# RWKV scan: wide operand products, 16-row inverses, a merge one group ahead and preparations between a group's halves

## The chip, the cores and the metric

The kernel runs on one core of one Trainium2 chip. The metric is the device time of one launch in microseconds (us). Matrix products run on TensorE (PE; its weight loads are PEld), elementwise work on VectorE (DVE), ScalarE (ACT) and GpSimd (POOL), transfers are issued by SyncE (SP).

## The reference, cut to what matters

The kernel computes four layers over 512 latent tokens and 256 context tokens of width 1024 in float32. The change touches one of them, the RWKV-7 mixer, and in it the scan over tokens, for 16 heads of 64 channels and for both directions:

```python
def step(S, inp):
    w_t, k_t, v_t, kk_t, a_t = inp[:5]
    sa = jnp.einsum('bhvk,bhk->bhv', S, -kk_t)
    S = (S * w_t[:, :, None, :] + sa[..., None] * (kk_t * a_t)[:, :, None, :]
         + v_t[..., None] * k_t[:, :, None, :])
    y = jnp.einsum('bhvk,bhk->bhv', S, inp[5]) if len(inp) == 6 else None
    return S, y
```

The context is scanned first and gives the start state of the latents; only latent steps give an output y. The kernel works in chunks of 64 tokens: within a chunk the steps become a unit lower triangular 64x64 system for each head, whose inverse is built once, and the state goes from chunk to chunk by matrix products.

## The kernel before

`rwkv_scan` handles 24 units. A unit is one direction d, one half h of the channels (8 heads, as 4 pairs on 128 partitions) and one stretch of 128 tokens (two chunks, j = 0 and 1): 8 systems of 2 heads. Units 0 to 7 are context, 8 to 23 latents. Two units (h = 0, 1) of the same direction make a pair; there are 12 pairs, and the direction alternates from pair to pair. Four steps make up the work:

- `prepare(g, d, h)` loads five operands (four for the context), runs a prefix sum on DVE (L1673), three exponentials on ACT, and the products of the operands with the decays on DVE: `W[.., 0]` (L1681, two of 64x512), `BK` (L1693 and L1694, eight of 64x256 for one unit, since each head's half is written into its own block of a zero-padded tile), `W[.., 1]` (L1697, latents only). Then, for j and for each two head pairs a0, eight matmuls (L1710, contraction over 128 partitions, half of them zeros) fill two PSUM banks, `pgB` and `pgK`, out of a ring of four; DVE takes them out under a mask (L1712 once, L1716 twice, 256 columns each for latents) and ACT takes out the rest (L1713, L1717). Last, ACT copies the 32x32 diagonal blocks, negated, to `diag` (L1719).
- `inverse(g, d)` transposes the pair's 32x32 blocks on DVE (L1726, 128x1024) and inverts them by forward substitution in `base_inverse`: 30 steps of two operations on POOL (L769, L770), or on DVE for pairs 1 and 11 (`n in (3, 23)`, n being the last unit of the pair).
- `merge(g, d, tv)` transposes the inverses twice on DVE (L1732, L1733, 128x1024), and builds the 64x64 inverse from the two 32x32 ones with 32 matmuls (L1742), a negation on ACT (L1744), copies on DVE and ACT (L1746), 32 matmuls (L1749) and copies on ACT (L1751).
- `consume(g, d, h, j)` is the recurrence: matmuls L1772, a copy on ACT (L1774), L1777, ACT (L1779), then L1786 and L1787 for the context or L1795 and L1796 for latents, the output on ACT (L1801), a transpose on PE (L1805) and the new state on DVE (L1782).

The operands of six units (`W`, `B`, `w`) are kept in a ring (`NS = 6`). Program order is written out at the end of `rwkv_scan`: after a start (units 0 to 4 prepared, pair 0 merged), each pair k is consumed, first j = 0 and then j = 1 for both units, then pair k+1 is merged, then units 2k+6 and 2k+7 are prepared and the pair of them goes to its inverse. A planner at compile time orders each engine's queue by the times that it estimates, with program order as the priority; on the chip each queue runs in that order. Units 0 and 1 are prepared while the projection of v still runs (its weights are split on POOL, L168); the other units come after it, from about 2596 us, when the tiles of the projection are free. The stage after the scan (`rwkv_out`) begins with the sum of the two directions' outputs (L1878).

Of the kernel before, what the change touches and what calls it, by code (L numbers as in the profile page):

```python
# [28 lines left out]
_CST = ["ident", "ones", "bd64", "cen"]  # L29
# [32 lines left out]
class K:  # L62
# [694 lines left out]

    def base_inverse(self, X, vector=False, pool=None):

        nc = self.nc  # L760
        v = X.rearrange("p (r c) -> p r c", r=32)
        nc.gpsimd.memset(X[:, 0:1024:33], 1.0)
        tt = nc.vector.tensor_tensor if vector else nc.gpsimd.tensor_tensor
        for k in range(1, 31):
            n = 31 - k
            t = (pool or self.pb).tile([128, 256], F32, name="binv", tag=f"binv{int(vector)}", bufs=2)
# [829 lines left out]
    def rwkv_scan(self):  # L1596
# [5 lines left out]
        pool = self.pb  # L1602
        reset, masks = self.cp[0], self.rr[1].rearrange("p (a b) -> p a b", a=2)
# [4 lines left out]
        i4 = lambda n, sh=None: pool.tile(sh or [128, 1024], F32, name=n, tag="i4", bufs=4)  # L1608
        BK = [pool.tile([128, 4, 2, 128], F32, name=f"BK{i}") for i in range(2)]

        diag = [pool.tile([128, 32, 32], F32, name=f"Ld{d}") for d in range(2)]
        X0 = pool.tile([128, 1024], F32, name="X0")
# [11 lines left out]
        for t in BK:  # L1624
            nc.gpsimd.memset(t, 0.0)
        for t in diag:
            nc.gpsimd.memset(t[:, 16:32], 0.0)
# [3 lines left out]
        for i, ch in enumerate((d, h) for d in range(2) for h in range(2)):  # L1631
            work[ch] = [g4[i], *h2((self.x[2:4] + self.cp[2:4])[i]), h2(self.x[4 + i // 2])[i % 2].rearrange("p a t -> p (a t)").rearrange("p (b h t) -> p b h t", b=2, h=2)]
# [8 lines left out]
        seen = set()  # L1641
# [4 lines left out]
        def prepare(g, d, h):  # L1646
# [3 lines left out]
            w4 = lambda hh, x: W[half[hh], :, x, hh, :]  # L1650
            src = lambda n, o: R[n][4 * h:4 * h + 4, :, o * 128:(o + 1) * 128].rearrange("c p t -> p c t")
            t = {}
            for n in (f"sig{d}", "kk", f"b{d}", f"kd{d}"):
                t[n[:2]] = e2("i" + n)
# [9 lines left out]
            W, B = s["W"], s["B"]  # L1664
            if 4 * g + 2 * d + h < NS:
# [3 lines left out]
            if not ctx and id(s) not in seen:  # L1669
                seen.add(id(s))  # L1670
                nc.gpsimd.memset(W[:, :, 1], 0.0)
# [7 lines left out]
            v4 = lambda x, hh: o(x[half[hh]]).rearrange("p (u t) -> p u t", u=8)  # L1679
            for hh in range(2):  # L1680
                nc.vector.tensor_tensor(out=w4(hh, 0), in0=v4(kk, hh), in1=v4(We, hh), op=ALU.mult)  # L1681
            nc.scalar.copy(s["w"].unsqueeze(2), u8(Wi)[:, :, 63:64])
            for j in range(2):
                k = 1 - j if d else j
                ts = slice(64 * k, 64 * k + 64)
                us = slice(j, 8, 2)
                bk = BK[nbk[0] % len(BK)]
                nbk[0] += 1
                r1 = (lambda x: x[:, ::-1, ::-1]) if d else (lambda x: x)
                r0 = (lambda x: x[:, ::-1]) if d else (lambda x: x)  # L1690
                for hh in range(2):
                    ps = half[hh]
                    nc.vector.tensor_tensor(out=bk[ps, :, hh, 0:64], in0=r1(b[ps, :, ts]), in1=r1(iW[ps, :, ts]), op=ALU.mult)  # L1693
                    nc.vector.tensor_tensor(out=bk[ps, :, hh, 64:128], in0=r0(kd[ps, :, ts]), in1=r0(iW[ps, :, ts]), op=ALU.mult)  # L1694
                if j == 0 and not ctx:
                    for hh in range(2):
# [298 lines left out]
def prep(I):  # L1995
    A = {}
# [164 lines left out]
```

## Time and profile before

| | us |
|---|---|
| median of 3 runs (3607.12 to 3620.38) | 3610.18 |
| profiled execution, its own time | 3611.94 |
| its span, first to last instruction | 3610.2 |
| the scan after the projection of v, 2596 to 3126 us of the span | 530 |

The profile's time and span are 1.7 us apart and within 0.05% of the median. Times in the rows below are microseconds from the start of the span unless marked ns. A row of the stretches gives its bounds and length, then for PE, PEld, DVE, ACT and POOL the busy time (x instructions), then the granted TensorE clock as a share of full speed, the busy share of the DMA engines and GB/s. A row of the grouped instructions gives line, engine, operation, tiles (out<-in), shape, count, then total busy time and the mean of one in ns, then the idle time of the engine before them and who ended it. A row of the timeline gives start, duration, engine, line, operation, tiles, shape and count, with the idle time before it in brackets.

### The profile page before, as it was taken

The page shows a single profiled execution, that of the slowest core. Times are in us where ns is not written, and L with a number is a line of the kernel's source. Part 1 is how long each engine was busy: PE and PEld are TensorE (multiplying, and loading weights), DVE is VectorE, ACT ScalarE, POOL GpSimd, SP SyncE. Part 2 cuts the span into 40 slices and gives each one's busy share as a digit, 9 for nine tenths or more (in the row PEclk, how much of TensorE's full clock was granted, in tenths as well). Part 3 has the DMA queues.
Part 4 walks back from the last instruction along what each step waited for, and adds up shares of the span by engine and source line. Part 5 has one row for each costly group of instructions (what it writes and reads, how often), then busy time and mean ns, then how long its engine had stood idle before and what let it go on. Part 6 is the DMA issues. An engine that isn't in the chain of part 4 may idle for free. (4 is left out here: it accounts for less than half of the span.)

```text
span 3610.2 us, 52987 instructions
## 1 busy us (share of the span) xinstructions
PE 3125.1 (87%) x20190; PEld 2483.5 (69%) x20190; DVE 2068.2 (57%) x3360; ACT 1446.5 (40%) x2766; POOL 1850.5 (51%) x1676
## 2 busy tenths in 40 slices
PE   5679895888989898999999998898867788789998
PEld 2258684766777686787888886665756667568886
DVE  7976845547667676674071415746489888540002
ACT  3247533333212446644212123356345555442223
POOL 6742631356556555534434334456647777165553
PEclk9789996999999899999999999888968888889999
DMA  6312357734332251122142512355412232412222
GB/s 218 122 64 72 114 206 238 216 115 142 120 108 99 82 164 47 32 75 88 59 175 94 179 68 81 115 200 200 126 51 82 73 80 75 152 58 100 99 95 81
DMA packets 265462, 412.14 MB, mean 114 GB/s; under 512 B 73716, under 2 KB 155252, under 8 KB 265208
## 3 DMA queue, kind: packets, MB, share of 16 engines
q1 hardware_dynamic: 265208, 408.75, 34.5%
q8 instruction: 160, 2.62, 0.3%
q14 instruction: 94, 0.77, 0.1%
HBM read 331.34 MB, written 70.25 MB: 111 GB/s over the span
## 5 line engine op out<-in xcount | busy, mean ns | idle before, releaser
L168 POOL TENSOR_TENSOR wlo<-wraw,whi 128x1024 fp32r<-128x1024 f32 (+1 forms) x269 | 660.2, 2456 | 897.6 <-ACT whi L172 871.4
L172 ACT CAST whi<-wraw 128x1024 fp32r<-128x1024 f32 (+1 forms) x269 | 278.1, 1036 | 862.1 <-PE pmm L192 760.4
L191 PE MATMUL pmm<-hxh,whi 128*128 128x512 f32 x1320 | 532.0, 406 | 20.3 <-ACT hxh L262 9.4
L192 PE MATMUL pmm<-hxl,whi 128*128 128x512 f32 x1320 | 532.3, 404 | 13.5 <-POOL hxl L168 13.5
L193 PE MATMUL pmm<-hxh,wlo 128*128 128x512 f32 x1320 | 529.3, 401 | 0.0
L284 DVE SCALAR_TENSOR_TENSOR mjunk<-mraw,cv 128x1024 bf16<-128x1024 f32 x224 | 351.5, 1569 | 62.8 <-DMA mraw<-in_mod_w 37.7
L191 PEld LDWEIGHTS pmm<-hxh,whi 128*128 128x128 f32 x1320 | 254.0, 193 | 80.3 <-ACT hxh L262 12.3
L192 PEld LDWEIGHTS pmm<-hxl,whi 128*128 128x128 f32 x1320 | 253.0, 192 | 72.9 <-POOL hxl L168 19.9
L193 PEld LDWEIGHTS pmm<-hxh,wlo 128*128 128x128 f32 x1320 | 253.6, 192 | 55.7 <-issue 0.7
L191 PE MATMUL pmm<-hch,whi 128*128 128x256 f32 x760 | 221.3, 291 | 9.9 <-ACT hch L262 6.5
L192 PE MATMUL pmm<-hcl,whi 128*128 128x256 f32 x760 | 220.5, 290 | 7.9 <-POOL hcl L168 7.8
L193 PE MATMUL pmm<-hch,wlo 128*128 128x256 f32 x760 | 220.1, 290 | 0.0
L1371 DVE TENSOR_TENSOR sg<-sg,pmm 128x512 f32<-128x512 f32 x44 | 30.2, 687 | 325.1 <-PE pmm L193 307.9
L770 POOL TENSOR_TENSOR X<-X,binv 128x30 f32<-128x30 f32 (+4 forms) x330 | 199.1, 604 | 23.9
L769 POOL TENSOR_TENSOR binv<-X 128x30 f32<-128x30 f32 (+4 forms) x330 | 187.7, 570 | 23.8
L191 PEld LDWEIGHTS pmm<-hch,whi 128*128 128x128 f32 x760 | 148.3, 195 | 19.8 <-ACT hch L262 8.9
L192 PEld LDWEIGHTS pmm<-hcl,whi 128*128 128x128 f32 x760 | 147.7, 194 | 16.4 <-POOL hcl L168 11.2
L193 PEld LDWEIGHTS pmm<-hch,wlo 128*128 128x128 f32 x760 | 148.3, 195 | 1.4 <-issue 0.8
L1710 PE MATMUL pgB<-W,BK 128*64 128x192 f32 (+1 forms) x768 | 106.5, 357 | 42.0 <-ACT B L1713 17.1
L191 PE MATMUL pmm<-lh,whi 128*128 128x512 f32 (+1 forms) x320 | 117.8, 370 | 23.1 <-ACT lh L1444 15.7
L191 PE MATMUL pmm<-hh,whi 128*128 128x512 f32 x352 | 137.8, 392 | 0.0
L192 PE MATMUL pmm<-hl,whi 128*128 128x512 f32 x352 | 137.8, 392 | 0.0
(546 smaller groups left out, 7639.9 us busy)
## 6 DMA issues: line engine op xcount, KB each, us to landing
mraw<-in_mod_w SPq DMA_DIRECT2D x96, 512.0 KB, 3.5
wraw<-in_wg SPq DMA_DIRECT2D x44, 512.0 KB, 3.4
wraw<-in_wu SPq DMA_DIRECT2D x44, 512.0 KB, 3.4
wraw<-in_e_w_in SPq DMA_DIRECT2D x32, 512.0 KB, 3.3
wraw<-in_o_w_in SPq DMA_DIRECT2D x32, 512.0 KB, 3.2
wraw<-in_wd SPq DMA_DIRECT2D x32, 512.0 KB, 3.4
mraw<-in_e_mod_w SPq DMA_DIRECT2D x24, 512.0 KB, 3.9
mraw<-in_o_mod_w SPq DMA_DIRECT2D x24, 512.0 KB, 5.1
```

Of the source, the lines that this page charges most:

```text
L168: self.nc.gpsimd.tensor_tensor(out=out, in0=in0, in1=in1, op=op)
L172: self.nc.scalar.copy(hi, src)
L191: nc.tensor.matmul(ps, lhsT=a[0], rhs=b[0], start=start, stop=False)
L192: nc.tensor.matmul(ps, lhsT=a[0], rhs=b[1], start=False, stop=False)
L193: nc.tensor.matmul(ps, lhsT=a[1], rhs=b[0], start=False, stop=stop)
L284: nc.vector.scalar_tensor_tensor(out=junk, in0=raw, scalar=1.0, in1=cv, op0=ALU.mult, op1=ALU.mult, accum_out=out[:, c:c + 1])
L769: tt(out=tv, in0=v[:, k + 1:, k:k + 1].to_broadcast(sh), in1=v[:, k:k + 1, :k].to_broadcast(sh), op=ALU.mult)
L770: tt(out=v[:, k + 1:, :k], in0=v[:, k + 1:, :k], in1=tv, op=ALU.add)
L1371: nc.vector.tensor_tensor(out=t, in0=t, in1=ps, op=ALU.mult)
L1710: nc.tensor.matmul(view(p)[half[q], a], lhsT=bk[:, a0 + a, hh, o:o + 64], rhs=rhs, start=True, stop=True)
```

## The change

1. **Operand products.** `BK` becomes one unpadded tile for a unit; eight DVE products of 64x256 become two of 128x512. The zero fills of `W`, `BK` and `diag` on POOL go.
2. **Fills.** The matmuls that fill `pgB` and `pgK` contract over 64 partitions only; a tile takes two banks and holds all four head pairs, and the ring of four single banks becomes two double ones. For each j, 16 matmuls, then one masked product of B and two of W on DVE, each 512 columns wide for latents, and three copies on ACT.
3. **Inverse.** The substitution runs on 16x16 blocks: `base_inverse(..., 16)` takes 14 steps on POOL, for all pairs, on tiles of 256 columns. Ahead of it stand a DVE transpose of 128x512 and one DVE operation that picks blocks.
4. **Merge.** Two ACT copies, two DVE transposes of 128x512, then 160 added matmuls of 32x32x32 in three rounds, with four DVE operations between and behind them that build the 32x32 inverses from the 16x16 ones. The steps from 32 to 64 stay.
5. **Consume.** The first product is eight matmuls of 64 columns that need no extraction of diagonal blocks (one ACT copy less); the order of the latents' last product alternates the halves of the output.
6. **Order.** The merge of pair k+2 is emitted between the two halves of pair k+1, one group earlier; the preparation of unit 2k+6 stands ahead of the first half of pair k+1 and that of 2k+7 behind the merge.
7. Loads of `sig` and `kk` get a ring of their own (four buffers beside five). A constant block (`sub`, 128x128) is added to one load at the start.

```diff
-    def base_inverse(self, X, vector=False, pool=None):
+    def base_inverse(self, X, vector=False, pool=None, m=32):
...
-        for k in range(1, 31):
-            n = 31 - k
+        for k in range(1, m - 1):
+            n = m - 1 - k
...
-        BK = [pool.tile([128, 4, 2, 128], F32, name=f"BK{i}") for i in range(2)]
+        BK = [pool.tile([128, 2, 8, 64], F32, name=f"BK{i}") for i in range(2)]
...
-                nc.gpsimd.memset(W[:, :, 0:3:2], 0.0)
...
+            bk = BK[nbk[0] % len(BK)]
+            tt(out=pj(bk[:, 0]), in0=run(b), in1=run(iW), op=ALU.mult)
+            tt(out=pj(bk[:, 1]), in0=lie(kd), in1=lie(iW), op=ALU.mult)
+            if not ctx:
+                for hh, q in enumerate(half):
+                    tt(out=pj(w4(hh, 1)), in0=run(r)[q], in1=run(Wi)[q], op=ALU.mult)
...
             for j in range(2):
+                pB, pK = self.bank("g", "pgB"), self.bank("g", "pgK")
+                vB, vK = (p.rearrange("p (a x) -> p a x", a=4) for p in (pB, pK))
+                for a in range(4):
+                    u = 2 * a + j
+                    for i, p in enumerate((vB, vK)):
+                        for hh in range(2):
+                            nc.tensor.matmul(p[half[hh ^ i], a, 0:n], lhsT=bk[half[hh], i, u], rhs=W[half[hh], u, 0:3:step, hh], start=True, stop=True)
+                bu = B[:, j:8:2]
+                tt(out=bu[:, :, 0:64 * sm], in0=vB[:, :, 0:64 * sm], in1=m4(masks[:, 0]), op=ALU.mult)
+                nc.scalar.copy(bu[:, :, 128:192], vB[:, :, 64 * sm:n])
                 for hh in range(2):
-                    nc.vector.tensor_tensor(out=bk[ps, :, hh, 0:64], in0=r1(b[ps, :, ts]), in1=r1(iW[ps, :, ts]), op=ALU.mult)
-                    nc.vector.tensor_tensor(out=bk[ps, :, hh, 64:128], in0=r0(kd[ps, :, ts]), in1=r0(iW[ps, :, ts]), op=ALU.mult)
...
+                    q = half[1 - hh]
+                    tt(out=W[q, j:8:2, 0:sm, hh, :], in0=x64(vK[q, :, 0:64 * sm]), in1=x64(m4(masks[q, d])), op=ALU.mult)
+                    nc.scalar.copy(W[q, j:8:2, 2, hh, :], vK[q, :, 64 * sm:n])
...
         def inverse(g, d, vector=False):
-            nc.vector.transpose(out=xv, in_=diag[d].rearrange("p u c -> p c u"))
-            self.base_inverse(X, vector, pool)
+            nc.vector.transpose(out=Xt, in_=by(diag[d]))
+            nc.vector.scalar_tensor_tensor(out=X, in0=Xt[:, :, 0:16], scalar=even, in1=Xt[:, :, 16:32], op0=ALU.mult, op1=ALU.add)
+            self.base_inverse(X.rearrange("p r c -> p (r c)"), vector, pool, 16)
...
+        def merge(g, d, X):
+            for b, m in enumerate((even, odd)):
+                nc.scalar.activation(out=z[:, :, 16 * b:16 * b + 16], in_=X, func=AF.Copy, scale=m)
+            nc.vector.transpose(out=by(U), in_=z)
+            nc.vector.transpose(out=flat(Tc), in_=flat(U))
+            for u in range(16):
+                for q, _ in blk:
+                    nc.tensor.matmul(v16(pa)[q, u], lhsT=diag[d][q, u], rhs=Tc[q, u], start=True, stop=True)
+            tt(out=Y1, in0=v16(pa), in1=corner.unsqueeze(1).to_broadcast([128, 16, 32]), op=ALU.mult)
+            for u in range(16):
+                for q, _ in blk:
+                    nc.tensor.matmul(v16(pb)[q, u], lhsT=Y1[q, u], rhs=U[q, u], start=True, stop=True)
+            for u in range(16):
+                for q, _ in blk[::2]:
+                    nc.tensor.matmul(v16(pc)[q, u], lhsT=U[q, u], rhs=Y1[q, u], start=True, stop=True)
+            for q, _ in blk[::2]:
+                tt(out=Tc[q], in0=Tc[q], in1=v16(pc)[q], op=ALU.add)
+            tt(out=U, in0=U, in1=v16(pb), op=ALU.add)
...
-                nc.tensor.matmul(p4[:, a], lhsT=W[:, u, 0].rearrange("p h t -> p (h t)"), rhs=hv[:, a].rearrange("p h e -> p (h e)"), start=True, stop=True)
+                for hh, q in enumerate(half):
+                    nc.tensor.matmul(p4[q, a], lhsT=W[:, 2 * a + j, 0, hh], rhs=hv[:, a, hh], start=True, stop=True)
...
-                    tv[n // 2] = inverse(*pair(n // 2), n in (3, 23))
+                    tv[n // 2] = inverse(*pair(n // 2))
...
         for k in range(12):
-            for j in range(2):
-                for n in (2 * k, 2 * k + 1):
-                    consume(*unit(n), j)
...
-            join(k + 1)
             ahead(2 * k + 6)
+            both(k + 1, 0)
+            join(k + 2)
             ahead(2 * k + 7)
+            both(k + 1, 1)
...
-    with k.phase("rwkv_b", "right"), k.psum("ps_g", g=4):
+    with k.phase("rwkv_b", "right"), k.psum("ps_g", g=(2, 2)):
```

`ahead(n)` prepares unit n and, for odd n, issues the pair's inverse; `join(n)` merges pair n; `both(k, j)` consumes half j of pair k.

## Rows read from the trace of the kernel before

**Rows 1.** Busy time of each engine in four stretches of the scan.

```profile
2596.00:2708.00 112.00, 66.74 (x1040) 56.18 (x1040) 95.33 (x219) 59.21 (x172) 49.21 (x83) 0.70 0.26 71
2708.00:2800.00 92.00, 72.11 (x1040) 60.21 (x1040) 85.38 (x152) 50.93 (x147) 67.31 (x111) 0.84 0.30 82
2800.00:3064.00 264.00, 212.07 (x2788) 172.75 (x2788) 223.41 (x384) 149.50 (x440) 206.94 (x355) 0.88 0.29 76
3064.00:3126.00 62.00, 51.25 (x820) 46.08 (x820) 37.12 (x87) 29.39 (x81) 5.33 (x15) 0.89 0.39 117
```

**Rows 2.** Grouped instructions of DVE, shapes apart, 2800 to 3064 us.

```profile
L1716 DVE TENSOR_TENSOR W<-pgK,r 64x256 f32<-64x256 f32 x96 | 40.2, 420 | 18.0 <-PE pgK L1710 10.1 <-ACT W L1717 5.9
L1694 DVE TENSOR_TENSOR BK<-ikd,x 64x256 f32<-64x256 f32 x44 | 27.2, 618 | 0.8 <-PE pgK L1710 0.7
L1693 DVE TENSOR_TENSOR BK<-ib,x 64x256 f32<-64x256 f32 x44 | 23.9, 542 | 8.4 <-ACT x L1678 7.7
L1712 DVE TENSOR_TENSOR B<-pgB,r 128x256 f32<-128x256 f32 x48 | 20.1, 420 | 2.5 <-PE pgB L1710 1.3 <-PE pch L1795 0.2
L1681 DVE TENSOR_TENSOR W<-ikk,isig 64x512 f32<-64x512 f32 x22 | 18.7, 848 | 1.2 <-PE pch L1772 1.0
...
L1746 DVE COPY B<-Uc 32x256 f32<-32x256 f32 x24 | 14.8, 618 | 0.4
...
L1732 DVE STREAM_TRANSPOSE Tc<-X 128x1024 f32<-128x1024 f32 x6 | 12.5, 2080 | 0.2
```

**Rows 3.** The same view, 2620 to 2660 us, where POOL is almost at rest.

```profile
L1716 DVE TENSOR_TENSOR W<-pgK,r 64x128 f32<-64x128 f32 x20 | 5.7, 287 | 0.5
L1693 DVE TENSOR_TENSOR BK<-ib,x 64x256 f32<-64x256 f32 x10 | 4.2, 417 | 0.3
...
L1681 DVE TENSOR_TENSOR W<-ikk,isig 64x512 f32<-64x512 f32 x3 | 2.2, 720 | 0.0
...
L1746 DVE COPY B<-Uc 32x256 f32<-32x256 f32 x4 | 1.1, 286 | 0.1
```

**Rows 4.** Timeline of DVE behind the scan: a 128x512 product that reads PSUM.

```profile
3146.42 0.69 DVE L1852 TENSOR_TENSOR rstd<-rstd,pyc 128x512 f32<-128x512 f32 x1 [4.47 <-ACT rstd L1887]
```

**Rows 5.** Grouped instructions of DVE, 2596 to 3126 us: the two inverses that run there.

```profile
L769 DVE TENSOR_TENSOR binv<-X 128x30 f32<-128x30 f32 (+14 forms) x60 | 24.1, 402 | 1.7
...
L770 DVE TENSOR_TENSOR X<-X,binv 128x30 f32<-128x30 f32 (+14 forms) x60 | 22.8, 380 | 1.7
```

**Rows 6.** Waits of DVE, 2596 to 2708 us: total, times, longest.

```profile
DVE Tc L1732 <- POOL X L770: 7.2, 1, 7.2
DVE W L1681 <- POOL W L1666: 5.4, 2, 5.1
```

**Rows 7.** Grouped instructions of POOL, shapes apart, 2800 to 3064 us.

```profile
L770 POOL TENSOR_TENSOR X<-X,binv 128x58 f32<-128x58 f32 x12 | 6.1, 508 | 0.9
...
L769 POOL TENSOR_TENSOR binv<-X 128x30 f32<-128x30 f32 x12 | 3.9, 341 | 0.5
```

**Rows 8.** Timeline of PE at the full granted clock: fills, and bursts of small products.

```profile
2845.76 0.33 PE L1710 MATMUL pgB<-W,BK 128*64 128x192 f32 x1
2845.77 0.33 PE L1710 MATMUL pgK<-W,BK 128*64 128x192 f32 x1
2845.92 0.33 PE L1710 MATMUL pgB<-W,BK 128*64 128x192 f32 x1
...
3093.28 0.68 PE L1777 MATMUL pch<-x,B 64*64 64x64 f32 x16
...
3100.06 1.20 PE L1742 MATMUL pmg<-Tc,B 32*32 32x32 f32 x64 [0.49 <-DVE Tc L1732]
```

**Rows 9.** Timeline of DVE and PE in the tail of the scan.

```profile
3061.89 1.97 DVE L1726 STREAM_TRANSPOSE X<-Ld 128x1024 f32<-128x1024 f32 x1
...
3097.93 2.07 DVE L1732 STREAM_TRANSPOSE Tc<-X 128x1024 f32<-128x1024 f32 x1
...
3104.81 3.78 PE L1772 MATMUL pch<-HV,W 128*128 128x128 f32 x16 [1.70 <-ACT B L1751]
```

More of the change, by code (lines that the diff above doesn't have):

```diff
@@ L28 @@
 ]
-_CST = ["ident", "ones", "bd64", "cen"]
+_CST = ["ident", "ones", "bd64", "cen", "sub"]
 _MAGIC = 12582912.0
@@ L1764, in consume @@
             PP = (PA, PB)
+            y, G5 = (t.rearrange("p (b h) e -> p b h e", b=2) for t in (y, G))
             p = self.bank(f"q{d}{h}", "pch")
[L1766 to L1772 removed]
@@ L1773, in consume @@
-            for hh, q in enumerate(half):
-                nc.scalar.copy(G[q], p4[q, :, 64 * hh:64 * hh + 64])
-            for a, u in pairs:
-                for q in half:
-                    nc.tensor.matmul(s4[q, a], lhsT=B[q, u, 0:64], rhs=G[q, a], start=True, stop=True)
-            for hh, q in enumerate(half):
-                nc.scalar.mul(PP[hh][q], s4[q], -1.0)
-            def state(p):
+            p4 = p[:, 0:256].rearrange("p (a e) -> p a e", a=4)
+            for a in range(4):
+                for hh, q in enumerate(half):
+                    nc.tensor.matmul(p4[q, a], lhsT=W[:, 2 * a + j, 0, hh], rhs=hv[:, a, hh], start=True, stop=True)
@@ L1781, in state @@
+            nc.scalar.copy(G, p4)
+            for a in range(4):
+                for q in half:
+                    nc.tensor.matmul(p4[q, a], lhsT=B[q, 2 * a + j, 0:64], rhs=G[q, a], start=True, stop=True)
+            for hh, q in enumerate(half):
+                nc.scalar.mul(PP[hh][q], p4[q], -1.0)
+            def state():
                 for hh, q in enumerate(half):
-                    nc.vector.tensor_tensor(out=nx[q, :, hh, :], in0=p[q], in1=w[q].unsqueeze(2).to_broadcast([64, 4, 64]), op=ALU.mult)
+                    tt(out=nx[q, :, hh, :], in0=p4[q], in1=s["w"][q, j::2].unsqueeze(2).to_broadcast([64, 4, 64]), op=ALU.mult)
@@ L1836, in rwkv_scan, with both @@
         ahead(4)
-        for k in range(12):
-            for j in range(2):
-                for n in (2 * k, 2 * k + 1):
-                    consume(*unit(n), j)
-                if k == 0 and j == 0:
-                    ahead(5)
-            join(k + 1)
+        def both(k, j):
+            for n in (2 * k, 2 * k + 1):
+                if n < 24:
+                    consume(*unit(n), j)
+        both(0, 0)
+        join(1)
+        ahead(5)
+        both(0, 1)
+        for k in range(12):
             ahead(2 * k + 6)
+            both(k + 1, 0)
+            join(k + 2)
             ahead(2 * k + 7)
+            both(k + 1, 1)
     def rwkv_out(self, ml):
@@ L2073, in prep @@
     same = r // 64 == q // 64
-    A["cst"] = _f(np.stack([r == q, one, same, (r == q) - same / 64.0], 1).astype(np.float32))
+    sub = np.where(q < 32, (r % 32 >= 16) & (q < 16), np.where(q < 34, r % 2 == q % 2, False))
+    A["cst"] = _f(np.stack([r == q, one, same, (r == q) - same / 64.0, sub], 1).astype(np.float32))
     A["tri"] = _f(np.stack([r <= q, r >= q, r < q, r > q], 1).astype(np.float32))
```

128 lines of the change are left out of this document (50 added, 78 removed).

## The prediction

> **What bounds the kernel now.** I read the busy times by stretch first, then the grouped instructions of the busiest engine. The scan after the projection of v takes 530 us, and in its first three stretches (468 us) DVE is busy 95.3, 85.4 and 223.4 us: 85, 93 and 85% [rows 1]. PE has 80% of the third stretch, POOL 78%, ACT 57%. PE's share there is no floor: the busy time includes each burst's run-out, and the granted clock averages 0.88, a mix of the 1.2 and 2.4 GHz levels. So the scan is bound by DVE with some waits between. The third stretch is the steady one: 96 masked products L1716, 16 to a pair, make it 6 pairs [rows 2], so a pair costs 264/6 = 44.0 us, of which DVE works 37.2 and stands 6.8. Where DVE stands, it waits at L1716 for a fill of PE (10.1 us in the stretch) or for ACT to leave the bank (5.9), and at L1693 for an exponential (7.7) [rows 2]. The last stretch is different: one chain runs through the last inverse, on DVE, to the last products [rows 9].
>
> DVE's price for a product of two SBUF tiles depends on POOL: 417 ns for 256 columns and 720 for 512 where POOL is nearly at rest, 542 to 618 and 848 where it is busy 78%; a copy is 286 against 618 ns [rows 2, 3]. Products that read PSUM are 420 ns for 256 columns in the busy stretch [rows 2] and 690 for 512 [rows 4].
>
> **The change, part by part.** The sums are made against the profiled execution (3611.94 us; the median is 1.8 lower, which I neglect).
>
> *Operand products.* In the steady stretch 88 products L1693 and L1694 take 51.1 us [rows 2]. They belong to 11 units and become 22 of 128x512. POOL's work falls (next part) to about 35% of the time, and I put a 512-column product between 720 and 848 ns, nearer the first, at 780: 17.2 us, so -33.9. The 44 products like L1681 that stay (848 ns) come to 780 as well: -3.0. Copies L1746, 24 of 618 ns, come to some 440: -4.3.
>
> *Masks.* 96 L1716 and 48 L1712 take 60.3 us [rows 2]; 72 of 512 columns at 690 ns [rows 4] take 49.7: -10.6.
>
> *Inverse.* POOL's 60 operations for a pair become 28 on 14 to 56 columns; by the rows of 30 and 58 columns (341 and 508 ns) [rows 7] 28 x 0.43 and gaps make about 14 us, against 206.9/6 = 34.5 now [rows 1]. On DVE a transpose of 1024 columns (2.0; L1732 has 2080 ns) [rows 2] becomes one of 512 (1.0) and an operation on 256 columns (0.5): -0.5 for a pair, -3 in the stretch. For pairs 1 and 11 DVE loses the whole substitution, 24.1 + 22.8 = 46.9 us, half of it each [rows 5].
>
> *Merge.* Two transposes of about 2.0 us become two of 1.0, and four operations of 512 columns that read PSUM come in, 4 x 0.69: +0.8 for a pair, +4.8 in the stretch. PE gets 160 matmuls more for a pair; a float32 matmul leaves two records, and 64 records of this size take 1.20 us [rows 8], so 320 take 6.0, or 3 if four quadrants run at once. DVE waits for PE twice in each merge, with PE waiting for DVE between; behind it in DVE's queue stand masks and states. The two new copies on ACT wait for POOL's last step, and behind them exponentials and evacuations queue. What covers that is half a group of consume, a preparation and another half, over 20 us, against 15 for transpose and substitution. I cost these waits at 0 to 4 us a pair and keep 1.
>
> *Fills and consume on PE.* A pair has now 128 fill records in column pairs, each pair of records 0.16 us apart [rows 8]: 10.3 us. With 64 rows a quarter of the array does a matmul; if four run at once it is 5.2, if two, still 10.3. The first product of consume and its copy shrink; I cost them at nothing, for PE (212 of 264) and ACT (149.5) stand behind DVE [rows 1]. Without that cover, PE's sum would count; that is the slower rival below.
>
> *The bank ring.* One fill at a time fits instead of two half ones, so PE can't fill for the next j until DVE and ACT have left both tiles. I take 0.2 us more idle DVE for each of the four j of a pair, together with the merge about 1.2 us a pair. Ends: 0, and 4 us for each j (second rival).
>
> *Order, loads, zero fills.* The merge a group ahead takes PE's wait for the transposes off the path of consume; since DVE is the bound that pays nothing by itself. The loads of a preparation move ahead of consume's v loads on SP; those go to tiles that are free a group earlier. The extra constant is one load of 64 KB more at the start: 0 to 0.3 us.
>
> *Steady stretch.* -33.9 - 3.0 - 4.3 - 10.6 - 3 + 4.8 = -50 us of durations. The durations of the stretch overlap a little (busy time is 96% of their sum), so -48; with 6 x 1.2 idle more, **-41**: a pair at 37.2 us.
>
> *Stretch 2708 to 2800.* It prepares five units, the same work at 73% POOL: by unit (the steady stretch holds 11 to 12) -48/11.5 x 5 = -21, less idle, **-17**.
>
> *Stretch 2596 to 2708.* Half of the 46.9 us [rows 5] goes, -23. Context units have half the columns and POOL is often idle: for a pair 16 operand products at about 0.45 become four at 0.72 (-4.2), 24 masks at 0.287 [rows 3] become 12 at 0.42 (-1.8); three pairs, -18, the merge about 0. DVE's waits for the late substitution on POOL, 7.2, and for the zero fills, 5.4 [rows 6], have no cause left: -12. That makes -53; with DVE out of the way the chain of preparation, inverse, merge and consume has less cover there than anywhere, so I give back a quarter: **-40**.
>
> *Tail.* From the last transpose (3061.9) it is 36 us to the merge's first (3097.9) and 6.9 more to the first product (3104.8) [rows 9]. After: transpose and pick 1.5, POOL 14, merge about 13: 28 instead of 43, and a first product with fewer columns streamed: **-16**.
>
> Sum: 41 + 17 + 40 + 16 = 114, so 3612 - 114 = **3498 us**.
>
> **The rivals.** *DVE closes up.* The next unit's products fill all waits and the fills run four at once: idle falls to 4 us a pair instead of 8. That is another 6 x 4 in the steady stretch and some 20 in the two before: **3452**. For it: DVE was at 93% in one stretch [rows 1]. Against it: ACT and PE come nearer to DVE in load.
>
> *The ring of two.* Each j is a closed loop: fill (16 matmuls, 32 records in pairs, 2.6 us and 0.3 of run-out), mask of B, mask of W, ACT, mask of W, ACT, next fill. DVE works 2.1 us in it and stands about 4 if its queue holds nothing else. Full exposure makes a pair (37.2 - 8 + 1) + 16 = 46, over the 44.0 of now: with the gains of the first stretch and the tail partly kept, about **3600**, no change that can be told. Half exposure costs about 50 us of the 114: **3548**. For it: the fill is already the first thing DVE waits for at L1716 [rows 2]. Against: 20 us of other DVE work in each pair can stand in these gaps.
>
> *PE becomes the bound (slower).* If matmuls on the two row halves of one bank took turns, 128 fill records at 0.16 would cost 20.5 us a pair instead of 10.3, the 320 new records of the merge 12.0 (64 of L1742, two at a time, take 1.20, so one has 0.0375 to itself), and the rest of PE's 212.1/6 = 35.3 busy us 23: 55 us a pair on PE, over the 44 of now. Six pairs +66, the latent pairs before +15, less about 30 kept at both ends: **3660**. It decides as soon as fills and merge cost PE more than 44 - 23 = 21 us a pair; with pairs at once they cost 16. Against it: L1777 works on two row halves of one bank. A record of 192 columns holds its tile for 0.16 us, so one of 64 columns for 0.053; its 16 records one after another would take 0.85 and a run-out of some 0.2, in pairs 0.43 and 0.2, and they took 0.68 [rows 8]. The Trainium skill, TensorEngine Tiling (Array Packing), Restrictions and Gotchas, states that different row tiles cannot access the same PSUM bank simultaneously; by that rule the time would be this rival's. The trace of L1777 does not agree with it.
>
> *The change doesn't do what it says*: the merge a group ahead finds its inverse unfinished and holds ACT. That is a few us a pair and lies within the half exposure.
>
> **How the numbers follow.** Forecast (3465 to 3530) 0.55; closing up 0.15; half exposure 0.18; full exposure or no change 0.06; PE bound 0.06. The range holds 8 in 10: from 3445 to 3565, that is the first three but for their outer ends. A difference under 0.5% (18 us) can't be told from none in this kernel. Faster by more than that (below 3592): 0.88; same 0.06; slower 0.06.
>
> **What would show it.** Steps right: 48 products of about 0.78 us in the place of L1693 and L1694; masks of 512 columns at 0.69; POOL busy near a third in the steady part; no substitution on DVE; the time between the last masks of successive pairs near 37 us with DVE at 80% or more; the tail from the last transpose to the end near 45 us instead of 63. Wrong: DVE under 70%, waiting at the masks for PE (ring of two), or PE's fills one matmul after another and PE over 95% (slower rival); new waits of ACT for POOL or of DVE for ACT at the merge.

## The result: slower, and the profile after

The changed kernel takes 3635.5 us (median of 5 runs, 3628.6 to 3640.6) against 3614.6 for the kernel before, a ratio of 1.0059 with a 95% interval of 1.0037 to 1.0081: slower by 21 us, where 114 us less were forecast. The profiled execution is the one of 3628.6 us. First its page: the span, the busy times, and the costliest group of the scan.

```profile
span 3626.8 us, 60562 instructions
...
PE 3114.1 (86%) x24414; PEld 2476.1 (68%) x24414; DVE 1921.9 (53%) x3012; ACT 1418.5 (39%) x2598; POOL 1590.0 (44%) x1396
...
L1701 PE MATMUL pgB<-W,BK 64*64 64x192 f32 (+1 forms) x768 | 96.0, 381 | 44.0 <-ACT B L1704 23.1
```

Then the stretches of [rows 1] (PE, PEld, DVE, ACT, POOL busy, with instructions; granted clock; DMA share; GB/s):

```profile
2596.00:2708.00 112.00, 69.49 (x1985) 61.27 (x1986) 66.01 (x121) 54.03 (x133) 19.52 (x58) 0.67 0.36 90
2708.00:2800.00 92.00, 62.22 (x1656) 52.35 (x1660) 56.38 (x96) 42.54 (x108) 21.52 (x58) 0.74 0.26 71
2800.00:3064.00 264.00, 194.13 (x4523) 158.53 (x4516) 156.02 (x260) 127.73 (x338) 57.19 (x174) 0.83 0.28 73
```

The work has gone as meant: in the third stretch DVE is busy 156 us in place of 223, POOL 57 in place of 207. The time has not followed. DVE stands idle 108 us of 264, and PE, ACT and POOL have become idler too. The prices are in the grouped instructions of DVE and POOL, 2800 to 3064 us, to be laid beside [rows 2] and [rows 7]:

```profile
L1708 DVE TENSOR_TENSOR W<-pgK,r 64x512 f32<-64x512 f32 x42 | 28.9, 688 | 11.6 <-PE pgK L1701 5.5 <-ACT W L1709 5.3
L1680 DVE TENSOR_TENSOR W<-ikk,isig 64x512 f32<-64x512 f32 x24 | 16.6, 692 | 0.6
...
L1703 DVE TENSOR_TENSOR B<-pgB,r 128x512 f32<-128x512 f32 x21 | 14.4, 687 | 3.5 <-PE pgB L1701 2.2 <-PE pgK L1701 0.7
...
L1684 DVE TENSOR_TENSOR BK<-ib,x 128x512 f32<-128x512 f32 x11 | 7.5, 683 | 1.2 <-ACT x L1674 1.1
...
L769 POOL TENSOR_TENSOR binv<-X 128x14 f32<-128x14 f32 (+6 forms) x84 | 29.4, 350 | 6.1
L770 POOL TENSOR_TENSOR X<-X,binv 128x14 f32<-128x14 f32 (+6 forms) x84 | 27.4, 327 | 6.6
```

Where the time is lost shows in the waits of the same stretch (total, times, longest):

```profile
ACT Z L1730 <- POOL X L770: 35.8, 5, 8.5
DVE Uc L1731 <- ACT Z L1730: 34.4, 6, 9.4
ACT B L1763 <- DVE Uc L1749: 28.0, 6, 7.4
...
DVE x L1669 <- DMA isig<-rw_sig: 10.9, 5, 3.3
```

At the merge's first step ACT waits for POOL's last, DVE waits for ACT, and later ACT for the merge's last addition. None of these waits is in the kernel before in this size; there DVE's largest are 10.1 and 7.7 us [rows 2]. The timeline of one pair shows what they are part of (start, duration, engine, line). DVE first, then POOL and ACT between 2760 and 2774 us:

```profile
2758.59 1.04 DVE L1721 STREAM_TRANSPOSE Xt<-Ld 128x512 f32<-128x512 f32 x1 [0.94 <-ACT Ld L1711]
2759.74 0.48 DVE L1722 SCALAR_TENSOR_TENSOR X<-Xt,cst 128x256 f32<-128x256 f32 x1
...
2774.14 1.04 DVE L1731 STREAM_TRANSPOSE Uc<-Z 128x512 f32<-128x512 f32 x1 [2.56 <-ACT Z L1730]
...
2794.02 0.69 DVE L1739 TENSOR_TENSOR Y<-pmh,cst 128x512 f32<-128x512 f32 x1
...
2799.05 1.37 DVE L1748 TENSOR_TENSOR Tc<-Tc,pmi 32x512 f32<-32x512 f32 x2 [1.78 <-PE pmi L1746]
2800.46 0.69 DVE L1749 TENSOR_TENSOR Uc<-Uc,pmh 128x512 f32<-128x512 f32 x1
...
2802.40 0.69 DVE L1703 TENSOR_TENSOR B<-pgB,r 128x512 f32<-128x512 f32 x1
...
2805.23 1.04 DVE L1721 STREAM_TRANSPOSE Xt<-Ld 128x512 f32<-128x512 f32 x1
2806.38 0.48 DVE L1722 SCALAR_TENSOR_TENSOR X<-Xt,cst 128x256 f32<-128x256 f32 x1
```

```profile
2760.35 0.21 POOL L769 TENSOR_TENSOR binv<-X 128x14 f32<-128x14 f32 x1
...
2772.96 0.22 POOL L770 TENSOR_TENSOR X<-X,binv 128x14 f32<-128x14 f32 x1
...
2773.20 0.91 ACT L1730 ACTIVATE Z<-X,cst 128x256 f32<-128x256 f32 x2 [5.46 <-POOL X L770]
```

This is a closed loop. The pick L1722 starts the substitution (2760.3 to 2773.2, 13 us). Its end starts the merge, whose steps wait in each queue among fills and consume: from the first copy L1730 to the last addition L1749 28 us (2773.2 to 2801.2). The last mask L1703 of the next unit stands behind that addition in DVE's queue (2802.4). From it come the copies of the diagonal blocks on ACT, the transpose and the pick of the *next* inverse (2806.4), 5.8 us in all. 13 + 28 + 6 = 47 us, and the first transposes of the merges are 47.3 us apart (2679.2 to 3057.7, eight pairs), against 45.5 before (2760.0 to 3033.3, six). Followed back through its waits from 3060 to 2728 us, the changed kernel's chain holds 59 us of POOL, in six of its seven substitutions; the chain of the kernel before, from 3060 to 2802, holds none.

### The profile page after: what moved, and what is told of

Read it like the earlier page. It is cut to its first block, busy times and chain, and to the rows that moved or that the text cites. A ratio compares the mean times of both kernels' runs of the same rounds, so it can differ in the third digit from the quotient of the medians.

```text
span 3626.8 us, 60562 instructions
## 1 busy us (share of the span) xinstructions
PE 3114.1 (86%) x24414; PEld 2476.1 (68%) x24414; DVE 1921.9 (53%) x3012; ACT 1418.5 (39%) x2598; POOL 1590.0 (44%) x1396
## 5 line engine op out<-in xcount | busy, mean ns | idle before, releaser
L192 PE MATMUL pmm<-hxl,whi 128*128 128x512 f32 x1320 | 531.0, 403 | 13.8 <-POOL hxl L168 13.8
L193 PEld LDWEIGHTS pmm<-hxh,wlo 128*128 128x128 f32 x1320 | 252.8, 192 | 55.8 <-issue 0.7
L193 PE MATMUL pmm<-hh,wlo 128*128 128x512 f32 x352 | 137.3, 392 | 0.0
L1701 PE MATMUL pgB<-W,BK 64*64 64x192 f32 (+1 forms) x768 | 96.0, 381 | 44.0 <-ACT B L1704 23.1
```

The source lines that it names most:

```text
L192: nc.tensor.matmul(ps, lhsT=a[0], rhs=b[1], start=False, stop=False)
L193: nc.tensor.matmul(ps, lhsT=a[1], rhs=b[0], start=False, stop=stop)
L1701: nc.tensor.matmul(p[half[hh ^ i], a, 0:n], lhsT=bk[half[hh], i, u], rhs=W[half[hh], u, 0:3:step, hh], start=True, stop=True)
```

## The experiments

Ratios are to the kernel before, with a 95% interval in brackets. Theory A is that loop: since the merge of a pair is emitted ahead of the preparation that ends in the next inverse, inverse, merge and next inverse follow one another. Theory B is the prediction's ring of two full banks. Others (C to G) came with the results.

**Order undone.** The changed kernel with the main loop of before (the body of the loop on one line here).

```
-            ahead(2 * k + 6); both(k + 1, 0); join(k + 2); ahead(2 * k + 7); both(k + 1, 1)
+            both(k, 0); both(k, 1); join(k + 1); ahead(2 * k + 6); ahead(2 * k + 7)
```

> The changed kernel with the main loop of before: both halves of a pair's consume, then the merge of the next pair, then two preparations with the next inverse. Theory A (a loop of one pair: the substitution on POOL takes 13 us, the merge behind it 20 to 28 us from its first copy to its last addition, and the last mask of the next unit stands behind that addition in DVE's queue, then 6 us of mask, copies and transpose to the next inverse; together the 45 us of a pair): here the inverse has a whole pair of time before its merge, the loop is gone, a pair falls to 36 to 40 us and the kernel to 3560 to 3600 us. Theory B (the ring of two full banks exposes each fill, whatever the order): 3620 to 3650 us, as the changed kernel.

3613.2 us, ratio 0.9993 (0.998 to 1.0007). 22 us come back, so the order costs at least that; but the gain stops at the kernel before, under what A had put. Its merges are 44.9 us apart with DVE busy 140 of 220 us (2800 to 3020). So taking the loop away isn't the whole answer.

**Two lines exchanged.** The next inverse ahead of the merge (in the start too, for unit 5 and pair 1), all else as changed. The text below calls this the exchanged order.

```
-            join(k + 2)
             ahead(2 * k + 7)
+            join(k + 2)
```

> The changed kernel with two lines of its loop exchanged: the second preparation with its inverse stands ahead of the merge in place of behind it. Theory A (the loop inverse, merge, last mask, next inverse): the next inverse no longer stands behind the merge, the substitution runs beside a whole pair of work, and ACT's wait for POOL at the merge's first copy (21 us in 200) goes to under 3; 3550 to 3600 us. Theory B (ring of two): nothing changes, 3620 to 3650 us.

3575.0 us, 0.9895 (0.9873 to 0.9918): 60 us less than the changed kernel and 39 less than before. The waits of ACT from 2800 to 3064 us now begin

```profile
ACT isig L1671 <- DVE x L1669: 26.2, 8, 7.1
ACT W L1709 <- DVE W L1708: 18.3, 27, 3.0
ACT B L1704 <- DVE B L1703: 13.7, 17, 2.1
```

and the wait for POOL at L1730, 35.8 us in the changed kernel, is 2.5; merges are 40.1 us apart. Followed back from 3020 to 2720 us, the chain holds no POOL at all. A holds, B does not: the ring is the same.

**The order alone, in the kernel before.** The first diff of this section backwards, in the kernel before:

```
-            both(k, 0); both(k, 1); join(k + 1); ahead(2 * k + 6); ahead(2 * k + 7)
+            ahead(2 * k + 6); both(k + 1, 0); join(k + 2); ahead(2 * k + 7); both(k + 1, 1)
```

> The kernel before with only the new main loop (merge a group ahead, preparations between the halves of consume). Theory A (loop): its substitution of 34 us on POOL comes into a loop with the merge and the last masks, 34 + 20 + 6 = 60 us a pair or more against 44: 3720 to 3850 us. Theory B (the ring and the narrower fills lose the time, not the order): 3590 to 3630 us.

3671.0 us, 1.0151 (1.0135 to 1.0167). The order alone makes the kernel slower by 57 us, less than A's price. The timeline of DVE shows a shorter loop, with the merge's two transposes and the next inverse's one right behind each other, in every pair from 2686 us on:

```profile
2830.49 2.05 DVE L1732 STREAM_TRANSPOSE Tc<-X 128x1024 f32<-128x1024 f32 x1
2832.41 1.95 DVE L1733 STREAM_TRANSPOSE Uc<-X 128x1024 f32<-128x1024 f32 x1
2834.18 1.88 DVE L1726 STREAM_TRANSPOSE X<-Ld 128x1024 f32<-128x1024 f32 x1
...
2882.05 2.01 DVE L1732 STREAM_TRANSPOSE Tc<-X 128x1024 f32<-128x1024 f32 x1
```

The spacing is 50.7 us (2780.9 to 3085.3), not the 60 expected: the next inverse follows the merge's transposes, not its end, so the 20 us that I had put for the merge are not in this loop. The substitution takes 38 to 41 us here, the three transposes 6, and between the substitution's end and the merge's first transpose DVE works off up to 8 us of its queue.

**Half of each substitution left out**, in the changed order and in the exchanged one.

```
-        for k in range(1, m - 1):
+        for k in range(1, m // 2):
```

> The changed kernel with the second half of each substitution left out (7 of 14 steps of each 16-block inverse, so the inverses are incomplete). Theory A (the substitution lies in the loop of a pair): 6.5 us less for each of some 9 pairs and in the tail, 3565 to 3590 us. Theory B (ring of two): POOL is beside the path, 3620 to 3640 us; only the tail's 6 us go.

> The kernel with the next inverse ahead of the merge (3575 us), with the second half of each substitution left out (7 of 14 steps of each 16-block inverse, so the inverses are incomplete). In the changed kernel the same cut took 50 us. Theory A (the exchange took the substitution off the path): only the tail can gain, 3565 to 3580 us. If it still sets the pace: 3520 to 3540 us.

In the changed order 3585.3 us, 50 less than the changed kernel, and merges 43.8 us apart in place of 47.3: of some 5.5 us that each substitution lost, 3.5 show in the spacing. In the exchanged order 3563.0, 12 less, of which the tail explains 5 (its last substitution takes 4.7 us in place of 9.4). The same cut is worth four times as much where the loop is closed.

**The ring.** Fills of two column pairs in four tiles of one bank, as before, with masks of 256 columns; once in the exchanged order, once in the old one.

```
-            for j in range(2):
+            for j, a0 in ((j, a0) for j in range(2) for a0 in (0, 2)):
...
-    k.psum("ps_g", g=(2, 2))
+    k.psum("ps_g", g=4)
```

> The same kernel (next inverse ahead of the merge, 3575 us) with the fills of before: two of the four column pairs at a time in one bank each, so that four tiles rotate in place of two, and masks of 256 columns in place of 512 (12 of about 0.42 us for 6 of 0.69 us in a unit, 0.9 us of DVE more). Theory B (the ring of two is what is left between this kernel and the forecast; DVE's waits for fills are 19 us in 200): 3530 to 3555 us. Theory A with no ring: 3570 to 3600 us.

> The changed kernel with the main loop of before (3613 us) and with the fills of before (four half tiles of one bank). In that order two preparations stand one behind the other, and DVE waits 26 us in 200 for fills. Theory B (there the ring of two is the limit): 3565 to 3590 us. Else 3605 to 3630 us.

3585.1 us (0.9928, 0.9913 to 0.9944), 10 more than with the ring of two, and 3616.7 (1.0011, 1.0 to 1.0022), 3 more, both with intervals that touch those of the ring of two. Each run has 0.9 us more of masks for a unit as well, 22 us of DVE at most, so a cost of the ring of up to 12 or 19 us could hide behind it, but not the 20 us and more that B had put. B falls in both of these orders; in the changed order itself the half banks weren't run.

**The parts alone.** In the order of before, the products, masks, fills and consume without the new inverse, and the new inverse and merge without the products; in the exchanged order, all but the new inverse. The runs with the old inverse also take the loads of `sig` and `kk` from the ring of before and keep two substitutions on DVE.

```
changed kernel, old order:
-        inverse, merge, base_inverse(..., m=16), diag of 16 x 32
+        inverse, merge, base_inverse(..., m=32), diag of 32 x 32 of the kernel before
kernel before, old order:
-        inverse, merge, base_inverse(..., m=32), diag of 32 x 32
+        inverse, merge, base_inverse(..., m=16), diag of 16 x 32 of the changed kernel
exchanged order:
-        inverse, merge, base_inverse(..., m=16), diag of 16 x 32
+        inverse, merge, base_inverse(..., m=32), diag of 32 x 32 of the kernel before
```

> The changed kernel with the order of before and with the 32-block inverse and its merge of before: that is, the kernel before with the wide products, the full-bank fills and masks and the new consume alone. As forecast (some 50 us of DVE in the steady stretch, 40 in the two before, nearly all of it gained): 3520 to 3545 us. Rival F (half of DVE's work lies on the chain): 3560 to 3590 us. If the full-bank fills lose what the products gain: 3600 to 3630 us.

> The kernel before with the 16-block inverse and its longer merge alone, in the order of before. As forecast (nothing in the steady stretch, some 30 us in the first stretches and 16 in the tail): 3560 to 3580 us. Rival G (the longer merge stands in the chain of every pair, with 0.6 to 3 us each time PE waits for its own next instructions, which the changed kernel shows at whole multiples of 256 records): some 4 us more for each of 11 pairs, less the 30 to 46 us early and late, 3605 to 3640 us.

> The changed kernel with the next inverse ahead of the merge (3575 us), but with the 32-block inverse and the merge of before. Rival G (the 16-block merge costs more on PE than its shorter substitution gains once the inverse has a whole pair of time): 3535 to 3565 us. If the substitution of 34 us sets the pace again: 3590 to 3650 us.

In the old order 3605.6 us (0.9981, 0.997 to 0.9991) with the products alone and 3621.3 (1.0027, 1.0018 to 1.0036) with the inverse alone, beside 3612.0 for the kernel before: -6 and +9. Their sum, +3, is what both give together in the old order (-1, the first experiment) to within 4 us; the new order then adds 22. So the change adds up, and its largest expected gain, the products, is the one that is missing. In the run with the products alone DVE is busy 165 of 220 us (2800 to 3020) in place of 184, and the products cost more than in the changed kernel, with POOL, under the old inverse, busy 173 us:

```profile
L1689 DVE TENSOR_TENSOR W<-ir,Wi 64x512 f32<-64x512 f32 x20 | 19.6, 981 | 1.4 <-ACT Wi L1674 0.7 <-DMA ir<-rw_r 0.4
L1681 DVE TENSOR_TENSOR W<-ikk,isig 64x512 f32<-64x512 f32 x20 | 17.7, 885 | 3.7 <-ACT isig L1672 1.7 <-PE pch L1763 1.6
```

Two things more differ there: PE's granted clock is 0.78 in place of 0.87, and the chain, followed back from 3060 to 2760 us, holds 73 us of POOL, two of the old substitutions, where that of the kernel before holds none. How much each of them takes of the missing gain wasn't tested.

In the exchanged order the old inverse takes 3587.7 us (0.9928, 0.9913 to 0.9943), 13 more than the new one, between the two ranges expected and nearer to the second: POOL is busy 183 of 220 us, and the merges are some 42 us apart. So the new inverse gains where the old order showed a loss. And the order pays: 18 us with the old inverse (3605.6 to 3587.7) and 38 with the new (3613.2 to 3575.0), once the next inverse stands ahead of the merge.

**The kernel before with less DVE work and nothing else.**

```
-                for hh in range(2):
+                for hh in range(2) if j == 0 else ():
                     nc.vector.tensor_tensor(out=bk[ps, :, hh, 0:64], ...)
```

> The kernel before without the operand products of the second half of each unit (4 of 8 of the 256-column products with the decay, L1693 and L1694, so that the second half is filled from zeros): 96 of them, at 0.55 us 53 us of DVE. Theory E (DVE bounds the kernel before, as its 85% of the time say): 3560 to 3575 us. Rival F (it is bound by a chain of handoffs on which DVE has 132 of 258 us): half of that or less, 3585 to 3605 us.

3593.0 us (0.9946, 0.9931 to 0.9961), 19 less. L1693 and L1694 take 55.8 us over the whole scan in place of 104.8, so 49 us of DVE are gone and 39% of them came back as time. Some of that may be PE's, whose granted clock is 0.94 from 2800 to 3020 us in place of 0.87. That decides between E and F: the kernel before is not bound by DVE alone, though DVE is busy 85% of the steady stretch. Followed back through its waits from 3060 us, 258 us of its chain hold 132 of DVE, 48 of PE, 46 of ACT and 29 without a shown cause, in turn.

**What is next in the exchanged order.** Four trials from 3575 us; the last two have the six load buffers of the second.

```
-                    tv[n // 2] = inverse(*pair(n // 2))
+                    tv[n // 2] = inverse(*pair(n // 2), True)
```

```
-        e3 = ... tag="e3", bufs=4
+        e3 = ... tag="e3", bufs=6
```

```
             ahead(2 * k + 7)
-            join(k + 2)
             both(k + 1, 1)
+            join(k + 2)
```

```
             for q, c in blk:
+                if c.start:
+                    nc.vector.tensor_scalar(out=diag[d][q, 8 * h:8 * h + 8, :], in0=B[q, :, c], scalar1=-1.0, ...)
+                else:
                     nc.scalar.mul(diag[d][q, 8 * h:8 * h + 8, :], B[q, :, c], -1.0)
```

> The kernel with the next inverse ahead of the merge (3575 us), and every substitution on DVE in place of POOL (28 operations on 14 to 56 columns; DVE is busy two thirds of the time there). Theory A (with the exchange the substitution has left the path): nothing in the steady part, the tail some 9 us shorter, 3560 to 3580 us. Rival C (the substitution still sets the pace of a pair): 9 us less for each pair, 3480 to 3510 us.

> The same kernel (3575 us) with six buffers in place of four for the tiles of sig and kk, so that a unit's loads can be issued a unit earlier. The chain of waits has 22 us of load of sig in 295. Theory D (late loads are the next limit): 3550 to 3562 us. Else 3570 to 3580 us.

> The kernel with six load buffers (3566 us), with the merge behind the second half of consume in place of ahead of it, so that only one preparation stands between a merge and its first product. If the merge's 12 to 27 us are covered by that preparation: 3555 to 3575 us; if consume waits for it: 3580 to 3610 us.

> The kernel with six load buffers (3566 us), with two of the four narrow copies ahead of each inverse (L1711, on ACT 0.41 us each, 16 us of 295 on the chain) on DVE at about 0.29 us. If they lie on the path of each unit: 0.8 us less for each of 20 units, 3545 to 3558 us. Else 3560 to 3575 us.

The substitution on DVE: 3612.0 us (0.9997, 0.9987 to 1.0008), 37 *more*, which no theory had. Its 28 operations come to 5.5 us a pair on DVE,

```profile
L770 DVE TENSOR_TENSOR X<-X,binv 128x14 f32<-128x14 f32 (+6 forms) x56 | 11.1, 199 | 1.5
...
L769 DVE TENSOR_TENSOR binv<-X 128x14 f32<-128x14 f32 (+6 forms) x56 | 10.9, 195 | 1.5
```

four pairs in 200 us, but each substitution stretches over 12 to 20 us there, its operations standing among products, masks and steps of the merge (on POOL it took 11 to 13). PE's wait at L1759 for the merge's addition L1748 on DVE grows from 3.3 to 13.8 us in 220, and its granted clock is 0.77 in place of 0.87. Which of these weighs most stays open. Six load buffers: 3566.5 (0.9874, 0.9849 to 0.9899); the interval overlaps that of four buffers, so a gain of 8 us is likely and not shown. The merge last: 3591.6 (0.9937, 0.992 to 0.9953), 25 more than with it in the middle, as expected if consume waits for it; from 2720 to 3020 us ACT's wait for the merge's last addition (L1763 for L1749) is 25.4 us in place of 10.9, and PE's stops at consume's first product, without a shown cause, 11.4 in place of 5.2. The narrow copies shared with DVE: 3575.3 (0.9897, 0.9883 to 0.9912), no gain.

**Is it PE then?** Half of the last products of consume left out, in the exchanged order.

```
-                    for w in range(2):
+                    for w in (1,):
```

> The kernel with the next inverse ahead of the merge (3575 us) without the products of W with v in the last step of consume (half of the records of L1815, 39 of 233 us of TensorE's records in 200 us; the outputs and states lack that part). If TensorE bounds that kernel (83% busy): 5 to 6 us less for each of eight pairs, 3530 us or less. If handoffs share the pace (TensorE has 111 of 295 us of the chain): a third of that, 3555 to 3568 us.

3577.3 us (0.9907, 0.9885 to 0.993): nothing gained. The stretch 2800 to 3020 us of the exchanged kernel, and under it of this one:

```profile
2800.00:3020.00 220.00, 182.18 (x4366) 148.08 (x4364) 146.84 (x245) 123.55 (x328) 52.12 (x145) 0.87 0.30 79
```

```profile
2800.00:3020.00 220.00, 174.56 (x3992) 137.00 (x3990) 147.42 (x245) 119.12 (x318) 46.93 (x145) 0.81 0.31 81
```

374 records fewer, but the granted clock falls from 0.87 to 0.81, a larger part of the time at the 1.2 GHz level, and PE is still busy 175 us. The fall isn't one execution's: over the whole kernel the clock is 0.910 to 0.914 in the four executions without the products and 0.915 to 0.920 in the four with them. Whether the clock took back all of the saving, or the chain of handoffs left no use for it, wasn't tested.

**Do small products cost more than their time?** In the changed kernel PE stops inside its bursts with no engine to wait for. The timeline of PE:

```profile
2793.72 0.33 PE L1701 MATMUL pgB<-W,BK 64*64 64x192 f32 x2
2793.73 0.33 PE L1701 MATMUL pgK<-W,BK 64*64 64x192 f32 x2
2793.88 0.33 PE L1701 MATMUL pgB<-W,BK 64*64 64x192 f32 x2
...
2795.88 0.64 PE L1746 MATMUL pmi<-Y,Uc 32*32 32x32 f32 x30
2798.31 0.70 PE L1746 MATMUL pmi<-Y,Uc 32*32 32x32 f32 x33 [1.79 <-issue]
```

Two runs put eight times as many of the merge's first products into the kernel before: eight in a row into one place, and the whole set eight times over.

```
+                        for _ in range(8):
                             nc.tensor.matmul(pY[o + 32:o + 64, u], ...)
```

```
-                for u in range(8):
+                for u in 8 * list(range(8)):
```

> The kernel before with each of the merge's first small products (L1742) issued eight times in a row into the same place. By their own rate (64 records in 1.20 us) this is 8.4 us more for a pair: up to 3710 us. If TensorE is handed its instructions more slowly than it can run such small ones (256 records of matmuls and weight loads in 4 to 5 us, as in the changed kernel between two of its stops), 896 records more are 14 to 17 us a pair, 3760 to 3810 us, with stops of 1 to 3 us every 256 records in the merge.

> The kernel before with the whole set of the merge's first products (L1742) issued eight times over, in turn over its places, so that two always run side by side as in the kernel before. By their own rate, 64 records in 1.20 us, 448 records more are 8.4 us a pair: no more than 3715 us, and no stops. If TensorE's instructions come more slowly than it runs them: stops of 1 to 3 us at whole multiples of 256 records of matmuls and weight loads in these bursts, 256 records taking 4 to 5 us in all, 896 records more 14 to 17 us a pair, 3740 to 3800 us.

The first gave 3777.2 us, +164 or 13.7 us a pair, as the second theory said, but for another reason, as its timeline and that of the second run show:

```profile
2803.19 4.42 PE L1743 MATMUL pmg<-Tc,B 32*32 32x32 f32 x100
...
2904.80 2.31 PE L1743 MATMUL pmg<-Tc,B 32*32 32x32 f32 x82 [1.86 <-DVE Tc L1732]
```

```profile
2785.54 2.01 PE L1742 MATMUL pmg<-Tc,B 32*32 32x32 f32 x100
2789.93 2.88 PE L1742 MATMUL pmg<-Tc,B 32*32 32x32 f32 x100
...
2825.43 1.77 PE L1742 MATMUL pmg<-Tc,B 32*32 32x32 f32 x100 [1.13 <-DVE Tc L1732]
```

The granted clock of these bursts, in order, is 0.50 and 1.00 in one place, and 0.84, 0.50 and 1.00 spread. So a record takes 44 ns in one place and 29 spread at 1.2 GHz, and 28 and 18 at 2.4 GHz, run-out of the burst included, with no stop within these bursts: 1.5 to 1.6 times as much in one place, and the rest is the clock (0.73 from 2800 to 3020 us, 0.81 spread, 0.87 before). The spread run takes 3709.6 us, +96 or 8.0 us a pair: their own rate (8.4). The theory that such bursts cost twice their time falls.

## Why the prediction was wrong

**The step that failed first: order, and the merge's waits.** The prediction said of the order that "since DVE is the bound that pays nothing by itself", and costed the merge's waits "at 0 to 4 us a pair and keep 1", covered by "over 20 us, against 15". That looked only at what lies between an inverse and its own merge, and there the cover was too small: ACT reached the merge's first copy before POOL was done in five of six pairs, 7 us early on average (35.8 us). And it did not ask what lies *behind* the merge: the last masks of the next unit, and so the next inverse. The two together close the loop of 47 us. Nor does the order pay nothing: with the next inverse ahead of the merge it gains 18 to 38 us. The mechanism was written down, as the rival that the change doesn't do what it says, and mis-sized: "a few us a pair" was 7 (47.3 against 40.1 us with two lines exchanged), some 60 us in all. Of the signs of being wrong that the prediction named, two came true: DVE under 70% (59% of the third stretch, though not for waits at the masks for PE, 5.5 and 2.2 us), and the last, new waits of ACT for POOL and of DVE for ACT at the merge.

**The step that failed under it: a busy share taken for a bound.** "So the scan is bound by DVE" rested on 85, 93 and 85% [rows 1], and every term of DVE was counted at 0.96 of its duration. Measured, 49 us off DVE gave 19 us. All of the products and masks in the old order gave 6. The account that fits is that a product in a chain of fill, mask, copy, fill gives its time back only where DVE is the late one; for the products alone the clock and the old substitution are rivals to it that weren't separated.

**What held.** Masks at 0.69 us (0.687 and 0.688). The inverse on POOL at 14 us: 13. The merge's steps on DVE. DVE's price under a busy POOL, which was put too high for after: 0.68 to 0.69 us for 512 columns in place of the 0.78 chosen, with POOL busy 22%, not the third foreseen. DVE's busy time in the third stretch fell by 67 us where 48 were forecast; but the stretch now holds 5.25 pairs of masks in place of 6 (42 of L1708, eight to a pair), so for a pair it is 29.7 us in place of 37.2, 45 for six pairs. So the durations on DVE and POOL were about right, and the sum was still wrong by 135 us.

**The rivals.** The ring of two, full or half exposed, fell with the four half banks, in the two orders in which they ran. PE as the bound fell: two products of pgB, one in each row half, start within 0.01 us of each other in the same bank (in its two halves of partitions), with two of pgK 0.01 us behind (2793.72 above), four at once, and the next four 0.16 us later. The Trainium skill, TensorEngine Tiling (Array Packing), Restrictions and Gotchas, states that different row tiles cannot access the same PSUM bank simultaneously; the trace of L1701 does not agree.

**The tail** forecast 16 us less: from the last transpose of the last inverse to the last store of y it is 55.4 us (3088.7 to 3144.1) against 64.1 (3061.9 to 3126.0), so 9. The substitution took some 10 us, less than the 14 forecast, but from the merge's first transpose to the last pair's first product it is 25 (3101.4 to 3126.6) in place of 13, among steps of consume.

**What stays open.** The exchanged kernel, 3575 us, is still 77 over the forecast. Followed back through its waits from 3020 to 2720 us, PE has 111 us, DVE 88, ACT 46, loads 25 and time without a shown cause 23. Less PE work, more banks, shared copies gave nothing, more load buffers perhaps 8. No one of them alone was shown to set the pace. That a chain through all of them does is argued from this, not shown.

Both the exchanged order (3575) and the same with six load buffers (3566) beat the two kernels of this case.

## What to carry to other kernels

When a step is emitted earlier, follow the queue not only to the step that needs it, but on from it: if the work that starts its successor stands behind it, a loop closes whose length is the sum of the latencies in it, and no engine need be busy for it. Emit the start of a long step on an idle engine (here the next inverse) ahead of anything that waits for the last one. And before counting DVE's microseconds as time, take some away: an engine busy 85% in a chain of handoffs gave back two fifths.

## What the hardware showed that was not expected

- **PE stops for its own instructions, after whole multiples of 256 of them.** The stops of the changed kernel that the profile puts down to no other engine, of 0.9 us and more, lie 1274, 256, 1530, 1784, 1786, 1530, 1274, 2042 and 1784 records of matmuls and weight loads apart (2667.6 to 3036.7 us). With the semaphore instructions in PE's queue counted too it is 1281, 256, 1536, 1791, 1793, 1536, 1279, 2048 and 1792, that is 5, 1, 6, 7, 7, 6, 5, 8 and 7 times 256 to within 1. In the exchanged order ten of twelve such distances fit to within a tenth of 256; in the kernel before one of three does (15.0, 3.7 and 3.9 times). Waits of PE put down to issue come to 18.7 us from 2596 to 3060 us, to 27.4 in the exchanged order, where bursts of the 16-block merge follow closer, and to 4.7 in the kernel before. The transfers tell what PE waits for: all ten of the stops in the changed kernel end 1.2 to 1.5 us after a packet of 16,384 bytes of the instruction queue has landed, where an arbitrary moment of this stretch falls within 1.1 to 1.7 us behind such a packet about one time in eleven. So PE stood for its own instructions. That isn't what makes the changed kernel slower: the exchanged order has more of it. Nor do dense bursts alone bring it on: the spread run, at 100 records in 1.8 to 2.9 us, has three stops in its bursts from 2596 to 3060 us, 3.1 us in all.
- **Small products into one place** take 1.5 to 1.6 times as long as in turn over their places: 28 against 18 ns a record at the full granted clock, 44 against 29 at 0.50.
- **A fill of 192 columns on 64x64 tiles** starts four at a time, every 0.16 us at the full granted clock (2793.2 to 2794.7 us) and every 0.32 at 0.50 (2799.9 to 2801.0).
- **The granted clock differs between these kernels, and PE's busy time doesn't tell it.** From 2800 to 3020 us it is 0.87 before, 0.82 after, 0.81 with products left out, 0.78 with the new products alone, 0.77 with the substitution on DVE, and 0.94 in the kernel before with fewer operand products; PE is busy 175, 162, 175, 161, 175 and 178 of the 220 us. At 175 to 178 us busy it is anything from 0.77 to 0.94. What sets it isn't shown; where it is lower, PE's products take longer, so work taken off PE need not shorten PE's time.
